# Lo parts of weights in a decoder layer: three FFN units by VectorE, two projection products by transfers within the chip

## The chip, the cores and the metric

The kernel runs on one core of a Trainium2 chip. A core has a matrix engine (TensorE, PE in the profile; its weight loads are PEld), a vector engine (VectorE, DVE), a scalar engine (ScalarE, ACT), GpSimd (POOL) and SyncE (SP), and 16 transfer engines shared by all queues. Here SP issues plain loads, and POOL issues the transfers that add to what lies at their destination. Each engine works through its own instructions in order, and so does each queue. The metric is the device time of one execution in microseconds; the median of the runs is quoted.

## The reference

One decoder layer on x of 512 tokens x 1024, in float32:

```
u = rms_norm(h, ln_mix_pre);  proj = u @ w_in
merged = g0*(y_swa @ w_swa) + g1*(y_sb @ w_sb) + g2*(y_mem @ w_mem)
mix = merged @ w_out
h = h + rms_norm(mix, ln_mix_post)
u = rms_norm(h, ln_ffn_pre)
a = silu(u @ w_gate) * (u @ w_up)            # 1024 -> 2816
h = h + rms_norm(a @ w_down, ln_ffn_post)
```

The change lies in `mix = merged @ w_out` (1024 x 1024), in the two norms behind it, and in the first weights of `u @ w_gate`, `u @ w_up`.

## The kernel before

**Precision.** TensorE multiplies in a shorter float format (fp32r). Each operand is split into hi, its value cast to that format by ScalarE, and lo, the rest; a product is three matmuls (`mm3`, lines 175, 177, 178): hi x hi, and the two of hi and lo. `split` (lines 135, 136) makes hi with a ScalarE cast and lo with a VectorE subtraction. `split_dma` (lines 147 to 149) makes lo without VectorE: ScalarE casts hi and writes -hi into lo, and a transfer issued by POOL adds the weight to it, here read again from the weights in main memory.

**Seven products.** The large products use a Winograd form of Strassen's scheme: a 2 x 2 block product with seven instead of eight half-size products, named p1, p2, p5, p6, p3, p7, p4, with sums of weights and of activations as operands. Weight sums are formed by accumulating transfers (`wo_plus`, `g_plus`). Products share PSUM banks: p1, p6, p7, p4 add up in bank x; p5 and p3 in y; p2 has w. Between two of a bank, ScalarE copies the intermediate state (p1, p5, p6), and VectorE joins it with a later one (`mkp` in the trace).

**The projection stage** (`mix_mm`, `wo_split`; about 410 to 452 us). Each product is done for token halves i = 0, 1 (256 tokens: two tiles of 128), with 4 k x 3 matmuls of 512 columns. The weights' parts are wop7h, wop7l and so on; those of p6 and p3 lie in tiles named hi and lo. p2 and p3 get lo by `split_dma`, the others by `split`. The activations' parts (mah/mal, mbd, mqh/mql, mrh/mrl) come from VectorE and ScalarE too; VectorE also joins the branches (g) just ahead.

**The norms** (`mix(t)`, lines 1132 to 1141, per token tile t of 128). Two ScalarE squares with accumulation, products with a gain (mt), statistics on 128 x 1 operands (b_m, t_m, v_m, r_m), the residual (xr), two more squares, statistics again (b_h to r_h), and the result mt. They are written under a priority that moves them forward in the engines' orders. `turn(t)` transposes mt by TensorE (ut) and splits it into FFN operands B11, B21 (tiles 0, 1) and, with tiles 2 and 3, T1, N2, N22, T3, T4.

**The FFN's gate and up products** work on units (p, n): p one of seven products, n a pair of 128-column blocks. A unit is one weight load of 512 KB (gw), one hi/lo split of 128 x 1024 and 24 matmuls of 256 columns. The order begins (p1,0), (p2,0), (p1,1), (p1,2), (p2,1), (p2,2), (p5,0), (p6,0), (p5,1), (p3,0). Unit (p1,0) is split by VectorE; the next three, (p2,0), (p1,1), (p1,2), by `split_dma` (`f_split_dma`, set as the unit's "way"). Their transfers share POOL's queue with the sums of weights of p5, p6 and p3 (`g_plus`, line 1246), which wait for their loads and for each other.

**What sets the order.** A scheduler orders each engine's instructions from the program's order, priorities and its own view of the dependences. `after(x, y)` pins x behind y on the same engine without a semaphore; `behind` pins later casts and subtractions to a given pair.

Of the kernel before, what the change touches and what calls it, by code (L numbers as in the profile page):

```python
# [17 lines left out]
P = 128  # L18
# [14 lines left out]
class Stream:  # L33
# [24 lines left out]
    def ahead(self, load_to, split_to):  # L58
        while self.loaded <= min(load_to, len(self.units) - 1):
            u = self.units[self.loaded]  # L60
            for fn in u["load"]:
                fn()
            u["raw"] = u["src"]() if callable(u["src"]) else self.load(u["src"], u["n"])
            self.loaded += 1
        while self.have <= min(split_to, len(self.units) - 1):
            u = self.units[self.have]
            for fn in u["split"]:
                fn()
            u["hl"] = u.get("way", self.split)(u["raw"], u["n"])
            self.have += 1  # L70

    def later(self, us, fn):
# [31 lines left out]
def tile_kernel(ctx, tc, a):  # L104
# [27 lines left out]
    def split(raw, hi, lo, sign=1.0):  # L132

        if sign == 1.0:
            ins = nc.scalar.copy(hi, raw)  # L135
            lows = nc.vector.tensor_tensor(lo, raw, hi.bitcast(F32), op=ALU.subtract)  # L136
        else:
            ins = nc.scalar.mul(hi, raw, sign)
            lows = nc.vector.scalar_tensor_tensor(lo, raw, sign, hi.bitcast(F32), op0=ALU.mult, op1=ALU.subtract)
        if "behind" in st:  # L140
            after(ins, st["behind"][0])
            after(lows, st["behind"][1])
        return ins

    def split_dma(raw, hi, lo, src):
# [114 lines left out]
    def parts(name, t):  # L260
        h, l = ck(f"{name}h", F32R), ck(f"{name}l", F32R)
        split(t[:, :], h[:, :], l[:, :])
        return h, l
# [325 lines left out]
    def branch(b, c2, order):  # L589
        def gen(hi, lo):  # L590
            for i in range(2):
                c = 2 * c2 + i
                g = st[(f"g{b}", c)] if (f"g{b}", c) in st else quart[(b, c)]
                ps = dps(f"br{b}{c}")
                for k in range(4):
                    mm3(ps[:, :], cols((hi, lo), (i * 4 + k) * P, P), y[(b, k)], k == 0, k == 3)
                    yield 0.65
                with tc.high_priority():
                    nc.vector.tensor_tensor(g[:, :], ps[:, :], g[:, :], op=ALU.mult)
                if order == 0:  # L600
                    st[("acc", c)] = g
                    continue
                acc = st[("acc", c)]
                if order == 1:
                    nc.vector.tensor_tensor(acc[:, :], acc[:, :], g[:, :], op=ALU.add)
                    continue
                nc.vector.tensor_tensor(acc[:, :], acc[:, :], g[:, :], op=ALU.add)
                merged[c] = acc
                if c < 4:
                    if c % 2 == 0:  # L610
                        ma.append((ck(f"mah{c}", F32R), ck(f"mal{c}", F32R)))
                    sl = slice((c % 2) * 256, (c % 2) * 256 + 256)
                    split(acc[:, :256], ma[-1][0][:, sl], ma[-1][1][:, sl])
                    continue
                mbd.append(parts(f"mbd{c}", acc))
                nc.vector.tensor_tensor(acc[:, 256:], merged[c - 4][:, 256:], acc[:, 256:], op=ALU.subtract)

        return gen
# [423 lines left out]
    def wo_split(p, key, k):  # L1042
        if p not in ("p6", "p3"):
            hl = tuple(ck(f"wo{p}{x}{k}", F32R)[:, :] for x in "hl")
        else:
# [1 line left out]
                uid[0] += 1  # L1047
                st["wo_two"] = [wp.tile([P, 1024], F32R, tag=x, name=f"{x}{uid[0]}", bufs=4) for x in ("hi", "lo")]
            hl = tuple(x[:, (k % 2) * 512 : (k % 2) * 512 + 512] for x in st["wo_two"])
        if p in ("p2", "p3"):  # L1050
            j, h = (1, 0) if p == "p2" else (1, 1)
            split_dma(wsum[key][k][:, :], *hl, a["w_out"][:, h, 4 * j + k])
        else:
            split(wsum[key][k][:, :], *hl)
        wt[(p, k)] = hl

    def rstd_small(name, ss):
# [456 lines left out]
    for k in range(4):  # L1514
        wo_split("p6", "r", k)
    wo_plus("r", 1, 0)
    for i in range(2):
        mix_mm("p2", i)
    for k in range(4):
# [2 lines left out]
    mix_mm("p5", 0)  # L1522
    mix_mm("p6", 0)
    for k in range(4):
        wo_split("p7", "b", k)
        turned_d(k)
    mix_mm("p5", 1)
    mix_mm("p3", 0)
    table("natural_log_exp_and_others")
    with tc.high_priority():  # L1530
        tmp[0] = mix(0)
    for k in range(4):
        wo_split("p4", "r", k)
    for p, i in (("p6", 1), ("p7", 0), ("p3", 1)):
        mix_mm(p, i)
    first.close()
# [2 lines left out]
    def f_split(raw, n):  # L1539
# [5 lines left out]
                split(x[:, :], hi[:, i * 512 : (i + 1) * 512], lo[:, i * 512 : (i + 1) * 512])  # L1545
        else:
            split(raw[:, :n], hi[:, :n], lo[:, :n])
        return hi, lo

    def f_split_dma(raw, src):  # L1550
        uid[0] += 1
        hi = fp.tile([P, 1024], F32R, tag="hi", name=f"hi{uid[0]}", bufs=4)
        lo = fp.tile([P, 1024], F32R, tag="lo", name=f"lo{uid[0]}", bufs=4)
        split_dma(raw[:, :], hi[:, :], lo[:, :], src)
        return hi, lo

    fs = Stream(None, f_split, LOAD_AHEAD + 1)
# [44 lines left out]
            tmp[t] = mix(t)  # L1602

    mixed(1)
    for i, (p, n) in enumerate(seq[:4]):
        if i > 0:
            fs.units[i]["way"] = lambda raw, w, n=n, j=(0 if p == "p1" else 1): f_split_dma(raw, g_src(n, 0, j))
    fs.ahead(3, 0)
    mix_mm("p4", 0)
    mixed(2)  # L1610
    mix_mm("p7", 1)
    turn(0, tmp[0])
    fs.ahead(4, 3)
    mix_mm("p4", 1)
    turn(1, tmp[1])
    mixed(3)
# [116 lines left out]
```

## Time and profile before

| what | us |
|---|---|
| runs shown | 813.27, 814.96, 815.26 (median 814.96) |
| the profiled execution | 813.38 |
| its span, first to last instruction | 811.6 |
| TensorE busy in the span | 784.5 |
| VectorE busy | 630.6 |
| ScalarE busy | 474.9 |
| POOL busy | 103.4 |
| mean granted TensorE clock | 0.984 of full |

Rows of the time line read: start, duration, engine, line of the kernel, operation, output <- inputs, shapes, count of merged instructions, and in brackets the idle time of the engine before and what ended it. Rows of waits read: engine, line and what waited <- what was waited for: total us, times, longest. Rows of stretches (a:b) give length, then busy us and count for PE, PEld, DVE, ACT, POOL, the granted clock, the busy share of the transfer engines (up to rounding errors above 1) and GB/s. Durations of pipelined matmuls overlap; the distance of their starts is what each takes. Rows of transfers end with the median us from issue to landing, or with minimum, median and maximum. The profiled time, 813.38, is 1.58 below the median of the runs; sums made on the trace are compared with it.

### The profile page before, as it was taken

The page shows a single profiled execution, that of the slowest core. Times are in us where ns is not written, and L with a number is a line of the kernel's source. Part 1 is how long each engine was busy: PE and PEld are TensorE (multiplying, and loading weights), DVE is VectorE, ACT ScalarE, POOL GpSimd, SP SyncE. Part 2 cuts the span into 40 slices and gives each one's busy share as a digit, 9 for nine tenths or more (in the row PEclk, how much of TensorE's full clock was granted, in tenths as well). Part 3 has the DMA queues.
Part 4 walks back from the last instruction along what each step waited for, and adds up shares of the span by engine and source line. Part 5 has one row for each costly group of instructions (what it writes and reads, how often), then busy time and mean ns, then how long its engine had stood idle before and what let it go on. Part 6 is the DMA issues. An engine that isn't in the chain of part 4 may idle for free.

```text
span 811.6 us, 12844 instructions
## 1 busy us (share of the span) xinstructions
PE 784.5 (97%) x4851; PEld 697.1 (86%) x4851; DVE 630.6 (78%) x999; ACT 474.9 (59%) x879; POOL 103.4 (13%) x130
## 2 busy tenths in 40 slices
PE   9999999999999999999999649999999999999996
PEld 6899887877888898899877549999999999988885
DVE  6898976844688796977688749977676767898797
ACT  7566755644655566656846837545555555666673
POOL 1102110000000001001560120110000000205200
PEclk9999999999999999999999769999999999999999
DMA  8343355222324027258993994987767762759902
GB/s 297 131 149 102 117 187 177 73 83 58 102 76 105 27 64 222 41 140 271 188 241 93 312 194 120 290 229 199 190 178 189 180 173 89 173 134 220 214 0 104
DMA packets 46334, 124.37 MB, mean 153 GB/s; under 512 B 5152, under 2 KB 7088, under 8 KB 46272
## 3 DMA queue, kind: packets, MB, share of 16 engines
q1 hardware_dynamic: 32448, 86.66, 33.0%
q0 software_dynamic: 13536, 36.69, 24.2%
q8 instruction: 38, 0.62, 0.3%
q10 hardware_dynamic: 288, 0.20, 0.1%
q14 instruction: 24, 0.20, 0.1%
HBM read 119.86 MB, written 3.67 MB: 152 GB/s over the span
## 4 chain that ended last, share of the span: by engine, by line
PE 90%; DVE 3%; issue 3%; DMA 2%; POOL 1%; ACT 0%; SPq 0%; DVEq 0%; POOLq 0%; ACTq 0%
PE gx L178 5%; PE gx L175 5%; PE gx L177 5%; PE g L175 3%; PE g L178 3%; PE br L177 3%; PE br L175 3%; PE g L177 3%; PE br L178 3%; PE gy L178 3%; PE gy L177 3%; PE gy L175 3%; PE x L175 2%; PE x L178 2%; PE x L177 2%
## 5 line engine op out<-in xcount | busy, mean ns | idle before, releaser
L135 ACT CAST hi<-gw 128x1024 fp32r<-128x1024 f32 x74 | 77.0, 1050 | 76.5 <-DVE gw L1264 36.0
L136 DVE TENSOR_TENSOR lo<-gw,hi 128x1024 fp32r<-128x1024 f32 x74 | 89.9, 1224 | 33.9 <-ACT hi L135 33.9
L135 ACT CAST hi<-raw 128x1024 fp32r<-128x1024 f32 (+2 forms) x52 | 53.9, 1042 | 51.9 <-PE g L177 13.7
L136 DVE TENSOR_TENSOR lo<-raw,hi 128x1024 fp32r<-128x1024 f32 (+2 forms) x52 | 62.9, 1215 | 19.0 <-ACT hi L135 18.8
L1246 POOL DMA_DIRECT2D gw<-in_w_gu x27 | 23.8, 906 | 201.8 <-DMA gw<-in_w_gu 75.8
L178 PE MATMUL gx<-B11h,lo 128*128 128x256 f32 x88 | 26.8, 304 | 10.7 <-DMA lo<-in_w_gu 10.7
L135 ACT CAST hi<-r 128x1024 fp32r<-128x1024 f32 (+1 forms) x24 | 23.6, 983 | 19.8 <-PE y L178 5.3
L177 PE MATMUL x<-lo,lh 128*128 128x512 f32 x88 | 34.2, 389 | 0.0
L175 PE MATMUL x<-hi,lh 128*128 128x512 f32 x88 | 34.2, 389 | 0.0
L178 PE MATMUL x<-hi,ll 128*128 128x512 f32 x88 | 34.1, 389 | 0.0
L838 DVE TENSOR_TENSOR_SCAN p<-r,anew 128x512 f32<-128x512 f32 (+1 forms) x24 | 24.7, 1041 | 8.1 <-ACT r L195 7.6
L175 PE MATMUL gx<-B11h,hi 128*128 128x256 f32 x88 | 26.9, 306 | 3.9 <-ACT B11h L1175 3.9
L136 DVE TENSOR_TENSOR lo<-r,hi 128x1024 fp32r<-128x1024 f32 (+1 forms) x24 | 27.2, 1133 | 3.9 <-ACT hi L135 3.7
L135 ACT CAST hi<-qw 128x1024 fp32r<-128x1024 f32 x18 | 18.9, 1052 | 16.1 <-PE g L177 3.7
L136 DVE TENSOR_TENSOR lo<-qw,hi 128x1024 fp32r<-128x1024 f32 x18 | 22.0, 1222 | 8.2 <-ACT hi L135 8.2
L178 PEld LDWEIGHTS gx<-B11h,lo 128*128 128x128 f32 x88 | 18.6, 212 | 10.9 <-DMA lo<-in_w_gu 10.9
L135 ACT CAST hi<-bp 128x512 fp32r<-128x512 f32 x33 | 19.2, 621 | 13.5 <-PE y L178 4.8
L177 PE MATMUL gx<-B11l,hi 128*128 128x256 f32 x88 | 26.6, 303 | 0.0
L136 DVE TENSOR_TENSOR lo<-bp,hi 128x512 fp32r<-128x512 f32 x33 | 22.4, 714 | 4.6 <-ACT hi L135 4.4
L175 PE MATMUL gw<-B21h,hi 128*128 128x256 f32 x88 | 25.1, 285 | 0.0
L178 PE MATMUL gy<-N22h,lo 128*128 128x256 f32 x88 | 25.0, 284 | 0.0
L175 PE MATMUL gx<-T4h,hi 128*128 128x256 f32 x88 | 25.0, 284 | 0.0
(1024 smaller groups left out, 2979.5 us busy)
## 6 DMA issues: line engine op xcount, KB each, us to landing
gw<-in_w_gu SPq DMA_DIRECT2D x57, 512.0 KB, 5.4
gw<-in_w_gu POOLq DMA_DIRECT2D x27, 512.0 KB, 7.3
raw<-in_w_p SPq DMA_DIRECT2D x26, 512.0 KB, 4.0
qw<-in_w_p SPq DMA_DIRECT2D x15, 512.0 KB, 3.9
raw<-in_w_br SPq DMA_DIRECT2D x12, 512.0 KB, 3.8
bp<-in_w_dn SPq DMA_DIRECT2D x22, 256.0 KB, 8.5
r<-in_w_dn POOLq DMA_DIRECT2D x10, 512.0 KB, 8.4
qw<-in_w_p POOLq DMA_DIRECT2D x6, 512.0 KB, 7.5
```

Source lines behind the costliest of these rows:

```text
L135: ins = nc.scalar.copy(hi, raw)
L136: lows = nc.vector.tensor_tensor(lo, raw, hi.bitcast(F32), op=ALU.subtract)
L175: one = nc.tensor.matmul(out, lh, rh, start=start, stop=False, skip_group_check=True)
L177: nc.tensor.matmul(out, *two, start=False, stop=False, skip_group_check=True)
L178: st["product"] = nc.tensor.matmul(out, *three, start=False, stop=stop, skip_group_check=True)
L838: ins = nc.vector.tensor_tensor_scan(p[:, :w], left1[i][:, :w], anew[:, o : o + w], 0.0, op0=ALU.mult, op1=ALU.max)
L1246: nc.gpsimd.dma_start(gw[(n, key)][:, :], g_src(n, i, j), accum_op=ALU.add)
```

## The change

- The three FFN units (p2,0), (p1,1), (p1,2) are split by `split`: ScalarE casts hi, VectorE subtracts. While they are written, `st["late"]` holds the last instruction of the second token tile's norm, and the three subtractions are pinned behind it. `f_split_dma` and the units' own "way" are gone.
- Projection products p7 and p4: lo by `split_dma`, but the transfer reads the weight sum that already lies on the chip (SBUF to SBUF). p7's split is written ahead of p2's products and p4's ahead of tile 0's norm; before, both came behind.
- p2's lo goes from a transfer to VectorE. p3 keeps its transfer from main memory.
- p6's four splits are pinned behind the last split of the merged branches (`st["seam"]`, the pair for mbd7).

```diff
@@ class Stream, ahead
-            u["hl"] = u.get("way", self.split)(u["raw"], u["n"])
+            u["hl"] = self.split(u["raw"], u["n"])
@@ split
             after(lows, st["behind"][1])
+        if "late" in st:
+            after(lows, st["late"])
+        st["both"] = (ins, lows)
         return ins
@@ branch
                 mbd.append(parts(f"mbd{c}", acc))
+                st["seam"] = st["both"]
@@ wo_split
-        if p in ("p2", "p3"):
-            j, h = (1, 0) if p == "p2" else (1, 1)
-            split_dma(wsum[key][k][:, :], *hl, a["w_out"][:, h, 4 * j + k])
+        if p in ("p7", "p4"):
+            split_dma(wsum[key][k][:, :], *hl, wsum[key][k][:, :])
+        elif p == "p3":
+            split_dma(wsum[key][k][:, :], *hl, a["w_out"][:, 1, 4 + k])
         else:
             split(wsum[key][k][:, :], *hl)
+            if p == "p6":
+                for x, y in zip(st["both"], st["seam"]):
+                    after(x, y)
@@ the projection stage
     wo_plus("r", 1, 0)
+    for k in range(4):
+        wo_split("p7", "b", k)
     for i in range(2):
         mix_mm("p2", i)
...
     for k in range(4):
-        wo_split("p7", "b", k)
         turned_d(k)
     mix_mm("p5", 1)
     mix_mm("p3", 0)
     table("natural_log_exp_and_others")
+    for k in range(4):
+        wo_split("p4", "r", k)
     with tc.high_priority():
         tmp[0] = mix(0)
-    for k in range(4):
-        wo_split("p4", "r", k)
@@ the FFN's first units
     mixed(1)
-    for i, (p, n) in enumerate(seq[:4]):
-        if i > 0:
-            fs.units[i]["way"] = lambda raw, w, n=n, j=(0 if p == "p1" else 1): f_split_dma(raw, g_src(n, 0, j))
+    late = st["mixed"]
     fs.ahead(3, 0)
     mix_mm("p4", 0)
     mixed(2)
     mix_mm("p7", 1)
     turn(0, tmp[0])
+    st["late"] = late
     fs.ahead(4, 3)
+    st.pop("late")
```

The engines' orders move at three places. First POOL's queue between the projection and the FFN; wor and wob are the projection's weight sums, gw the FFN's weights, lo its lo parts. Before:

```order
L1040 DMA wor3_3924<-in_w_out 128x512
L1246 DMA gw147_4783<-in_w_gu 128x1024
L149 DMA lo156_4892<-in_w_gu 128x1024
L1246 DMA gw148_4785<-in_w_gu 128x1024
L1246 DMA gw149_4787<-in_w_gu 128x1024
L1246 DMA gw148_4785<-in_w_gu 128x1024
L1246 DMA gw153_4884<-in_w_gu 128x1024
L1246 DMA gw149_4787<-in_w_gu 128x1024
L149 DMA lo157_4897<-in_w_gu 128x1024
L149 DMA lo158_4902<-in_w_gu 128x1024
```

Now:

```order
L1044 DMA wor3_3924<-in_w_out 128x512
L152 DMA wop7l0_4525<-wob0_4190 128x512
L152 DMA wop7l1_4530<-wob1_4191 128x512
L152 DMA wop7l2_4535<-wob2_4192 128x512
L152 DMA wop7l3_4540<-wob3_4193 128x512
L152 DMA wop4l0_4651<-wor0_3921 128x512
L152 DMA wop4l1_4656<-wor1_3922 128x512
L152 DMA wop4l2_4661<-wor2_3923 128x512
L152 DMA wop4l3_4666<-wor3_3924 128x512
L1254 DMA gw147_4787<-in_w_gu 128x1024
L1254 DMA gw148_4789<-in_w_gu 128x1024
```

The three transfers of FFN lo parts are gone, and eight transfers of the projection stand ahead of all the FFN's sums.

Second VectorE's order around tile 0's norm. mkp60 and mkp61 are the joins of p3 for token halves 0 and 1, mkp50 that of p7 for half 0; mt, b_m, v_m, t_m, r_m, xr are the norm. Before:

```order
L136 TENSOR_TENSOR wop7l3_4616<-wob3_4193,wop7h3_4615 128x512
L1120 TENSOR_TENSOR mkp60_4595<-my0_4568,mkp60_4595 128x512
L1134 TENSOR_TENSOR mt01_4653<-mkp60_4595,bc_g_post1_4311 128x512
L1134 TENSOR_TENSOR mt00_4652<-mkp10_4439,bc_g_post0_4310 128x512
L1061 TENSOR_SCALAR b_m0_4658<-ssm0_4650 128x1
L136 TENSOR_TENSOR wop4l0_4685<-wor0_3921,wop4h0_4684 128x512
L1063 SCALAR_TENSOR_TENSOR v_m0_4659<-ssm0_4650,b_m0_4658 128x1
L136 TENSOR_TENSOR wop4l1_4689<-wor1_3922,wop4h1_4688 128x512
L136 TENSOR_TENSOR wop4l2_4693<-wor2_3923,wop4h2_4692 128x512
L1065 SCALAR_TENSOR_TENSOR t_m0_4660<-r_m0_4661,v_m0_4659 128x1
L136 TENSOR_TENSOR wop4l3_4697<-wor3_3924,wop4h3_4696 128x512
L1123 TENSOR_TENSOR mkp50_4581<-mkp50_4581,mx0_4426 128x512
```

Now:

```order
L136 TENSOR_TENSOR mrl3_4487<-g13_1866,mrh3_4486 128x256
L1128 TENSOR_TENSOR mkp60_4611<-my0_4584,mkp60_4611 128x512
L1131 TENSOR_TENSOR mkp50_4597<-mkp50_4597,mx0_4422 128x512
L1142 TENSOR_TENSOR mt01_4673<-mkp60_4611,bc_g_post1_4307 128x512
L1142 TENSOR_TENSOR mt00_4672<-mkp10_4435,bc_g_post0_4306 128x512
L1069 TENSOR_SCALAR b_m0_4678<-ssm0_4670 128x1
L1071 SCALAR_TENSOR_TENSOR v_m0_4679<-ssm0_4670,b_m0_4678 128x1
L1073 SCALAR_TENSOR_TENSOR t_m0_4680<-r_m0_4681,v_m0_4679 128x1
L1128 TENSOR_TENSOR mkp61_4716<-my1_4621,mkp61_4716 128x512
L1074 SCALAR_TENSOR_TENSOR r_m0_4681<-t_m0_4680,r_m0_4681 128x1
L1145 SCALAR_TENSOR_TENSOR xr00_4492<-mt00_4672,r_m0_4681,xr00_4492 128x512
```

The eight subtractions of wop7l and wop4l are gone; the join of p7 stands ahead of both mt products, and the join of p3's second half within the statistics. On TensorE p3 and p6 have changed places: p6's second half now comes ahead of p3's first. On ScalarE the eight casts and negations of p7 stand ahead of the copies of p5 and p6, and those of p4 ahead of tile 0's squares.

Third VectorE's order behind tile 1's norm, in tile 2's norm; B11l and B21l are FFN operands, lo156 to lo158 the lo parts of the three FFN units. Before:

```order
L1141 SCALAR_TENSOR_TENSOR mt11_4748<-xr11_4501,r_h1_4770,bc_g_fpre1_4317 128x512
L1176 TENSOR_TENSOR B11l0_3614<-ut00_4862,B11h0_3613 128x2x128
L1063 SCALAR_TENSOR_TENSOR v_m2_4824<-ssm2_4815,b_m2_4823 128x1
L1176 TENSOR_TENSOR B11l0_3614<-ut10_4918,B11h0_3613 128x2x128
L1065 SCALAR_TENSOR_TENSOR t_m2_4825<-r_m2_4826,v_m2_4824 128x1
L1066 SCALAR_TENSOR_TENSOR r_m2_4826<-t_m2_4825,r_m2_4826 128x1
L1176 TENSOR_TENSOR B11l1_3616<-ut00_4862,B11h1_3615 128x2x128
L1137 SCALAR_TENSOR_TENSOR xr20_4504<-mt20_4817,r_m2_4826,xr20_4504 128x512
```

Now:

```order
L1184 TENSOR_TENSOR B11l0_3614<-ut00_4866,B11h0_3613 128x2x128
L1071 SCALAR_TENSOR_TENSOR v_m2_4828<-ssm2_4819,b_m2_4827 128x1
L136 TENSOR_TENSOR lo156_4896<-gw146_4785,hi156_4895 128x1024
L1073 SCALAR_TENSOR_TENSOR t_m2_4829<-r_m2_4830,v_m2_4828 128x1
L1184 TENSOR_TENSOR B11l1_3616<-ut00_4866,B11h1_3615 128x2x128
L1074 SCALAR_TENSOR_TENSOR r_m2_4830<-t_m2_4829,r_m2_4830 128x1
L136 TENSOR_TENSOR lo157_4900<-gw150_4793,hi157_4899 128x1024
L1145 SCALAR_TENSOR_TENSOR xr20_4500<-mt20_4821,r_m2_4830,xr20_4500 128x512
L1145 SCALAR_TENSOR_TENSOR xr21_4501<-mt21_4822,r_m2_4830,xr21_4501 128x512
L1184 TENSOR_TENSOR B21l0_3618<-ut01_4867,B21h0_3617 128x2x128
L1069 TENSOR_SCALAR b_h2_4841<-ssh2_4820 128x1
L136 TENSOR_TENSOR lo158_4904<-gw151_4801,hi158_4903 128x1024
```

Two of the three new subtractions stand ahead of tile 2's residual (xr) and one within its second statistics; the part of B11 for the second token tile (B11l0 from ut10) has moved behind all three.

More of the change, by code (lines that the diff above doesn't have):

```diff
@@ L1547, in f_split @@
             split(raw[:, :n], hi[:, :n], lo[:, :n])
[L1548 to L1554, printed above, removed]
         return hi, lo
```

## The prediction

> **What bounds the kernel now.** I read the page first, then the waits of TensorE over the whole span, then the stretch with the largest wait in order of time.
>
> ```profile
> span 811.6 us, 12844 instructions
> PE 784.5 (97%) x4851; PEld 697.1 (86%) x4851; DVE 630.6 (78%) x999; ACT 474.9 (59%) x879; POOL 103.4 (13%) x130
> ...
> PE gx L178 <- DMA lo<-in_w_gu: 10.7, 1, 10.7
> PE gx L175 <- ACT B11h L1175: 3.9, 1, 3.9
> PE ut L1187 <- DVE mt L1141: 2.6, 2, 1.3
> ```
>
> TensorE is busy for 784.5 of 811.6 us, so only its waits and its slow stretches can be won. One wait of 10.7 us is larger than all others together: the third matmul of the FFN's unit (p1,1) waits for a lo part that comes by an accumulating transfer. In order of time, TensorE and then POOL's queue:
>
> ```profile
> 469.67 0.28 PE L177 MATMUL gx<-B11l,hi 128*128 128x256 f32 x1
> 480.62 0.58 PE L178 MATMUL gx<-B11h,lo 128*128 128x256 f32 x1 [10.67 <-DMA lo<-in_w_gu]
> 481.00 0.42 PE L175 MATMUL gx<-B11h,hi 128*128 128x256 f32 x1
> 486.48 0.36 PE L175 MATMUL gx<-B11h,hi 128*128 128x256 f32 x1
> 486.80 0.28 PE L178 MATMUL gx<-B11h,lo 128*128 128x256 f32 x1
> ...
> 466.37 1.75 POOL L1246 DMA_DIRECT2D gw<-in_w_gu  x2 [14.34 <-DMA gw<-in_w_gu]
> 470.21 2.09 POOL L149 DMA_DIRECT2D lo<-in_w_gu  x2
> ```
>
> The two late lo transfers stand in POOL's queue behind a weight sum that waits 14.34 us, are issued at 470.21, and the first lands when the matmul starts, at 480.62. After the wait the matmuls start 0.21 us apart until 486.48 (0.42 us each) and 0.12 us apart afterwards (0.28 us each). So the wait also costs about 23 matmuls x 0.09 = 2.1 us of slow clock.
>
> The Trainium skill (TensorE: Matmul & The Clock Gate, Part 1: The HAM clock gate) puts the fall to half clock after some 3.4 us without work and the return after as much work; the trace agrees in direction, with 5.9 us from 480.62 to 486.48. By that rule alone every new wait of several us ahead of the FFN would bring such a stretch again.
>
> **The change, part by part.** *FFN lo parts.* Three transfers of 512 KB and three ScalarE negations go; VectorE gets three subtractions instead.
>
> ```profile
> 447.89 1.06 ACT L148 ACTIVATE lo<-hi 128x1024 fp32r<-128x1024 f32 x1
> L136 DVE TENSOR_TENSOR lo<-gw,hi 128x1024 fp32r<-128x1024 f32 x74 | 89.9, 1224 | 33.9 <-ACT hi L135 33.9
> lo<-in_w_gu POOLq DMA_DIRECT2D x3, 512.0 KB, 12.4
> ```
>
> ScalarE loses 3 x 1.06, VectorE gains 3 x 1.22 (1.13 from start to start where instructions follow each other), and all three stand, by the order, inside token tile 2's norm. That takes the 10.7 us wait away, but what comes next is VectorE's chain of norms, to which the other edits add too.
>
> *Lo parts of p7 and p4 by transfers inside the chip.* VectorE loses 8 subtractions of 128x512, 0.69 us each by the row of that shape at 466.03 below. ScalarE gains 8 negations, and each product waits for four transfers of 256 KB. TensorE's dates for p7 and p4, and ScalarE's and the transfers' rows:
>
> ```profile
> 429.27 0.41 ACT L135 CAST mqh<-g 128x256 fp32r<-128x256 f32 x1 [1.26 <-DVE g L1092]
> 430.54 2.20 ACT L135 CAST wop7h<-wob 128x512 fp32r<-128x512 f32 x4
> 437.14 0.39 PE L175 MATMUL mx<-wop7h,mrh 128*128 128x512 f32 x1
> 442.58 0.39 PE L175 MATMUL mx<-wop4h,mbd4h 128*128 128x512 f32 x1
> DMA to landing us min/median/max: 4.3/6.4/6.6
> DMA to landing us min/median/max: 5.4/7.5/10.7
> 428.00:436.00 8.00, 8.00 (x35) 6.57 (x36) 6.10 (x14) 4.55 (x11) 0.00 (x0) 1.00 0.30 59
> 436.00:444.00 8.00, 8.00 (x37) 6.63 (x36) 7.25 (x18) 5.84 (x18) 0.00 (x0) 1.00 0.06 7
> ```
>
> The two landing rows are those of wop2l and of wob, 256 KB each. No transfer from SBUF to SBUF is in the trace. The nearest rows bound its landing by 4.3 and 10.7 us, and the long ones were taken where the transfer engines were full; here they stand at 0.30 and 0.06 of their time. I take 5.4. Then: ScalarE's last mqh, now near 429.9, ends at 430.2; four pairs of a cast (2.20 / 4) and a negation (half of 1.06, at half the width), together about 1.05 us, end at 431.3 to 434.4; the last lo lands at 439.8. TensorE, 0.9 us later than before (next edit), needs it for its fourth k, at 437.14 + 0.9 + 3 x 0.68 + 0.23 = 440.3 (12 matmuls are 2.72 us: p7,0 begins at 437.14, and p4 two products later at 442.58). p4's pairs follow three copies of about 0.5 us and end at 440.2; landing 445.6, needed at 442.58 + 0.9 + 2.27 = 445.75. Both are in time by tenths only: at the low bound (4.3) nothing changes, at 10.7 p7's k = 3 is 4.8 us late. The negations also hold back the copy of p5's bank, which p3 overwrites; the new order runs p6,1 ahead of p3,0, and the copy ends at 435.0 for a start of p3,0 at 435.3.
>
> The Trainium skill (DMA: Bandwidth & Descriptors, Anatomy of one DMA) gives about 2.0 us plus bytes at 436 GB/s, an estimate of 2.6 us for 256 KB. No row here is as short, and by that figure p7 and p4 would have 3 us to spare.
>
> *p6 behind the seam, p2 by VectorE.* p2's four subtractions (2.4 us in all) fall between 390 and 400, and cost nothing as long as VectorE is idle there; without that cover they would cost 2.4. p6's pin moves two of its four subtractions into a full stretch:
>
> ```profile
> 395.00:400.00 5.00, 5.00 (x24) 4.14 (x23) 3.78 (x8) 5.00 (x11) 4.39 (x6) 1.00 1.07 194
> 427.94 0.50 PE L178 MATMUL mx<-hi,mrl 128*128 128x512 f32 x1 [0.25 <-DVE mrl L136]
> ```
>
> VectorE already sets the pace there (TensorE waits 0.25 us for its mrl). Two subtractions of 0.60 from start to start more, and one of them offset by mbd5l having run earlier, makes TensorE 0.6 to 1.2 us late; I take 0.9, on every date up to 448.
>
> *The chain of norms.* These rows give its dates before; the sum is the walk of the new order with their durations.
>
> ```profile
> 436.23 1.29 DVE L1134 TENSOR_TENSOR mt<-mkp,bc_g_post 128x512 f32<-128x512 f32 x2 [0.92 <-ACT mt L1132]
> 440.90 1.41 DVE L1137 SCALAR_TENSOR_TENSOR xr<-mt,r_m,xr 128x512 f32<-128x512 f32 x2
> 448.03 1.03 PE L1187 MATMUL ut<-c_ident,mt 128*128 128x128 f32 x8
> 449.27 1.42 DVE L1137 SCALAR_TENSOR_TENSOR xr<-mt,r_m,xr 128x512 f32<-128x512 f32 x2
> 461.55 0.58 PE L175 MATMUL gx<-B11h,hi 128*128 128x256 f32 x1 [3.93 <-ACT B11h L1175]
> 461.67 1.40 DVE L1141 SCALAR_TENSOR_TENSOR mt<-xr,r_h,bc_g_fpre 128x512 f32<-128x512 f32 x2
> 466.03 0.69 DVE L1134 TENSOR_TENSOR mt<-mkp,bc_g_post 128x512 f32<-128x512 f32 x1 [1.27 <-ACT mt L1132]
> 471.71 1.42 DVE L1141 SCALAR_TENSOR_TENSOR mt<-xr,r_h,bc_g_fpre 128x512 f32<-128x512 f32 x2
> 476.04 0.42 DVE L1274 TENSOR_TENSOR aq<-gp,sg 128x256 f32<-128x256 f32 x1
> 486.32 0.69 DVE L1196 TENSOR_TENSOR t<-ut,ur 128x512 f32<-128x512 f32 x1 [9.86 <-PE ut L1187]
> 503.24 2.36 DVE L136 TENSOR_TENSOR lo<-gw,hi 128x1024 fp32r<-128x1024 f32 x2
> 504.51 0.39 PE L178 MATMUL gy<-N22h,lo 128*128 128x256 f32 x1
> ```
>
> Tile 0: VectorE now has p7's join ahead of the two mt products, so these wait for p7,0's end, 437.14 + 12 matmuls x 0.227 (439.86) + 0.9 and a handover: join 441.0, mt 441.6 instead of 436.23; the join of p3,1 falls in between too, and xr starts at 444.6 instead of 440.9. Though eight subtractions left this stretch, tile 0 is 3.7 us later. Tile 1: the join of p7,1 (TensorE done near 448.9) stands ahead of its statistics; xr at 452.8 instead of 449.27, 3.5 later. Tile 2: two new lo parts stand ahead of its xr and one behind, 3 x 1.13 = 3.4, of which about 1.7 is new waiting; its mt ends near 468.3 instead of 463.07, 5.2 later. Tile 3: before, it began at 466.03, 3.0 us behind tile 2's mt, since it waited for ScalarE; that slack takes up 2.4 of the 5.2, and mt ends at 475.9 instead of 473.13, 2.8 later.
>
> TensorE's first FFN unit goes on at about 466.3 instead of 461.55, 4.8 later, and, without the 10.7 us wait, its last transposes (ut of tile 3) done near 478.5 instead of 486.48: 8.0 us earlier. VectorE has, between mt of tile 3 and the first step behind those transposes, 3.3 us of work (473.13 to 476.46 before, inside the wait of 9.86), so it starts that step at 475.9 + 3.3 = 479.2 instead of 486.32: 7.1 us earlier. From there VectorE was full up to the lo part that ends at 504.4, for which TensorE's matmul at 504.51 waited a tenth. So VectorE binds, and the gain is its 7.1 us and not TensorE's 8.0. Behind 504 nobody in TensorE's row waits and all moves along.
>
> Sum against the profiled execution's own 813.38 us (span 811.6): 10.7 + 2.1 won, 4.8 given back because the FFN's first units start later, 0.9 more because VectorE and not TensorE sets the pace behind them (rounding 0.1): 7.1, so 806.3. The median of the three runs shown is 814.96, 1.6 above the profiled one; on it 807.9, and I predict **808**.
>
> **The rivals.** *The on-chip lo parts land late* (as wob's did: median 7.5, longest 10.7 us, in the row above). p7's margin of 0.5 us makes 5.9 the landing from which it decides; each us more is a us for TensorE, then for tile 0's norm and all behind it. At 7.5 it costs 1.6, at 10.7 4.8, and the result is 809.5 to 812.7. For it: the margins of tenths; four transfers in flight at once. Against it: transfer engines nearly idle.
>
> *VectorE does not bind.* If mt of tile 3 ends as early as before, 473.1, VectorE starts at 476.4 and 9.9 us are won: 805; if TensorE also keeps its clock, all of 12.8: 802. Against it is the order, which puts lo parts and joins ahead of the norms.
>
> *Slower.* One mechanism: the transfers inside the chip take as long as the FFN's did (12.4, the row above, though for 512 KB). p7's last k is then 12.4 - 5.9 = 6.5 us late. p4's lands at 440.2 + 12.4 = 452.6, needed, with p7's delay, at 445.75 + 6.5 = 452.25: 0.4 more. If the wait also lets the clock fall as before (2.1), that is 9.0 against the 7.1 won: 817. It decides from a landing of about 12.6 us without, or 10.5 with, the slow clock. Queueing on POOL, one after the other, would have to do this.
>
> *The wait only changes its name.* If a later FFN unit then waits for its weight sums, the dates stay: 815.
>
> ```profile
> 478.37 1.75 POOL L1246 DMA_DIRECT2D gw<-in_w_gu  x2 [6.06 <-DMA gw<-in_w_gu]
> gw<-in_w_gu POOLq DMA_DIRECT2D x8, 512.0 KB, 8.8
> 501.51 1.05 ACT L135 CAST hi<-gw 128x1024 fp32r<-128x1024 f32 x1
> ```
>
> Against it: even unmoved the last two sums of the first seven products land near 479.2 + 8.8 = 488, and ScalarE takes unit (p3,0)'s weights at 501.51, so 7.1 earlier at 494.4.
>
> **How the numbers follow.** 0.3%, 2.4 us, is about what a measurement here can tell from no change. Forecast 0.57 (own range 805 to 811: 0.9 and 5.4 at their bounds and 1.5 us of error in each norm); late transfers 0.18; VectorE free 0.12; slower 0.06; renamed 0.07. Faster than 812.5: 0.55 + 0.14 + 0.12 = 0.81; slower than 817.4: 0.04 of the slower case and 0.03 of the renamed one, which would add this change's lost tenths; within: the other 0.12. The range that leaves out 2 in 10 reaches from 803.5, inside the free case, to 813, past the late transfers.
>
> **What would show it.** Right: no wait on DMA lo in TensorE's waits; ut of tile 3 near 478; mt of tile 0 at about 441.6 behind the join of p7; waits of TensorE of some us on mt and B11 between 453 and 468; VectorE full from 479. Wrong: a wait of TensorE on the transfers wop7l or wop4l (the late rival); mt of tile 3 ending before 474 (VectorE free); a wait on weight sums before 500 (renamed); waits behind 504, which my walk assumes away.

## The result, and the profile after

The changed kernel takes 804.03 us (median of 4 runs, 803.20 to 804.67), the kernel before 814.12 us in its 4 runs (812.46 to 815.26). The ratio is 0.9877, with a 95% interval from 0.9855 to 0.9899. The forecast was 808, with a range from 803.5 to 813: the sign and the range hold, and the gain of some 10 us is larger than the 7.1 of the sum. The time lies only 0.5 us above the lower end of the range, which was there for a rival (VectorE does not bind), and below the 805 to 811 that the forecast gave for its own mechanism.

The profiled execution is the one of 804.03 us. From its page, the span, the busy times and the chain that ended last:

```profile
span 802.2 us, 12855 instructions
PE 782.9 (98%) x4851; PEld 695.0 (87%) x4851; DVE 631.1 (79%) x998; ACT 474.7 (59%) x880; POOL 103.4 (13%) x131
PE 89%; DVE 7%; ACT 2%; issue 2%; DVEq 0%; ACTq 0%
```

What TensorE waited for over the whole span (engine, line, what waited <- what for: total us, times, longest):

```profile
PE ut L1195 <- DVE mt L1149: 4.0, 2, 2.8
PE gx L180 <- DVE B11l L1184: 3.2, 1, 3.2
PE gw L178 <- ACT B21h L1183: 1.9, 1, 1.9
```

The wait of 10.7 us on a transfer is gone. No transfer stands in TensorE's list; what is left between 452 and 464 are waits for the norms: for mt, which is to be transposed, and for the FFN operands made from it. The chain that ended last runs, outside TensorE, through VectorE (7%) and ScalarE (2%), and no transfer stands in it.

TensorE in order of time: p7's first matmul, the FFN's first steps, and tile 3's transposes.

```profile
436.07 0.39 PE L178 MATMUL mx<-wop7h,mrh 128*128 128x512 f32 x1
463.51 0.58 PE L180 MATMUL gx<-B11l,hi 128*128 128x256 f32 x1 [3.17 <-DVE B11l L1184]
467.01 0.28 PE L180 MATMUL gx<-B11l,hi 128*128 128x256 f32 x1
474.49 1.04 PE L1195 MATMUL ut<-c_ident,mt 128*128 128x128 f32 x8
```

p7,0 starts 1.07 us earlier than before (437.14), where the prediction had it 0.9 later. The first FFN units go on at 463.51, 2.0 later than before (461.55), not 4.8. From there to 467.01 the matmuls start 0.21 us apart, afterwards 0.12. Tile 3's transposes begin at 474.49; in the kernel before they began at 485.48, 11.0 us later, and the prediction had them near 478.

VectorE's dates for the norms (tile 0's mt products, xr of tiles 0 and 1, the results mt of tiles 2 and 3, and the first step t behind tile 3's transposes):

```profile
439.59 1.29 DVE L1142 TENSOR_TENSOR mt<-mkp,bc_g_post 128x512 f32<-128x512 f32 x2
442.52 1.41 DVE L1145 SCALAR_TENSOR_TENSOR xr<-mt,r_m,xr 128x512 f32<-128x512 f32 x2
450.65 1.41 DVE L1145 SCALAR_TENSOR_TENSOR xr<-mt,r_m,xr 128x512 f32<-128x512 f32 x2
463.78 1.41 DVE L1149 SCALAR_TENSOR_TENSOR mt<-xr,r_h,bc_g_fpre 128x512 f32<-128x512 f32 x2
472.96 1.42 DVE L1149 SCALAR_TENSOR_TENSOR mt<-xr,r_h,bc_g_fpre 128x512 f32<-128x512 f32 x2
477.63 0.68 DVE L1204 TENSOR_TENSOR t<-ut,ur 128x512 f32<-128x512 f32 x1
493.86 2.36 DVE L136 TENSOR_TENSOR lo<-gw,hi 128x1024 fp32r<-128x1024 f32 x2
```

| date on VectorE, us | before | predicted | measured |
|---|---|---|---|
| mt products of tile 0 | 436.23 | 441.6 | 439.59 |
| xr of tile 0 | 440.90 | 444.6 | 442.52 |
| xr of tile 1 | 449.27 | 452.8 | 450.65 |
| mt of tile 2, end | 463.07 | 468.3 | 465.2 |
| mt of tile 3, end | 473.13 | 475.9 | 474.4 |
| first step t behind tile 3's transposes | 486.32 | 479.2 | 477.63 |

Every norm came later than before, as forecast, and every one 1.5 to 3.1 us earlier than forecast. The step t starts without any wait, 3.1 us after TensorE began the transposes for it. VectorE is late there, not TensorE. The step is 8.7 us earlier than before; the lo parts that ended before's chain at 503.24 start at 493.86, 9.4 us earlier, and 9.4 is what the span lost (811.6 to 802.2).

### The profile page after: what moved, and what is told of

It reads as the page before. It is cut to its first block, busy times and chain, and to the rows that moved or that the text cites. A ratio compares the mean times of both kernels' runs of the same rounds, so it can differ in the third digit from the quotient of the medians.

```text
span 802.2 us, 12855 instructions
## 1 busy us (share of the span) xinstructions
PE 782.9 (98%) x4851; PEld 695.0 (87%) x4851; DVE 631.1 (79%) x998; ACT 474.7 (59%) x880; POOL 103.4 (13%) x131
## 4 chain that ended last, share of the span: by engine, by line
PE 89%; DVE 7%; ACT 2%; issue 2%; DVEq 0%; ACTq 0%
PE gx L178 5%; PE gx L181 5%; PE gx L180 5%; PE g L178 3%; PE g L181 3%; PE g L180 3%; PE gy L178 3%; PE gy L181 3%; PE gy L180 3%; PE br L178 3%; PE br L180 2%; PE br L181 2%; PE x L178 2%; PE x L181 2%; PE x L180 2%
## 5 line engine op out<-in xcount | busy, mean ns | idle before, releaser
L135 ACT CAST hi<-gw 128x1024 fp32r<-128x1024 f32 x77 | 79.8, 1047 | 77.0 <-DVE gw L1272 36.5
L136 DVE TENSOR_TENSOR lo<-gw,hi 128x1024 fp32r<-128x1024 f32 x77 | 93.5, 1223 | 34.0 <-ACT hi L135 34.0
L135 ACT CAST hi<-bp 128x512 fp32r<-128x512 f32 x33 | 19.3, 620 | 13.4 <-PE y L181 4.8
L181 PE MATMUL gy<-T1h,lo 128*128 128x256 f32 x88 | 25.0, 284 | 0.8 <-DVE lo L136 0.8
L387 POOL DMA_DIRECT2D qw<-in_w_p x6 | 7.3, 1211 | 140.0 <-DMA qw<-in_w_p 46.6
L178 PE MATMUL gy<-T1h,hi 128*128 128x256 f32 x88 | 25.0, 284 | 0.2 <-ACT hi L135 0.2
```

The lines of the kernel that those rows point to most:

```text
L178: one = nc.tensor.matmul(out, lh, rh, start=start, stop=False, skip_group_check=True)
L181: st["product"] = nc.tensor.matmul(out, *three, start=False, stop=stop, skip_group_check=True)
L387: nc.gpsimd.dma_start(raw[:, :].rearrange("p (g m) -> p g m", g=2), q_src(b, n, f, j), accum_op=ALU.add)
```

## The experiments

Eleven more kernels ran. One number orders them: the date of VectorE's step t, 477.63 in the rows above. The table gives the median, the ratio to the kernel before measured beside it (its medians were 814.12, 813.13, 813.93 and 813.34), the span of the profiled run and that date. The ratios of the change, e1, e4, e5 and e7 lie within each other's intervals: what sets these five apart is read from their traces, one for each kernel, and not from their times.

| kernel | median us | ratio, 95% interval | span | step t | span - t |
|---|---|---|---|---|---|
| before | 814.12 | 1 | 811.6 | 486.32 | 325.3 |
| the change | 804.03 | 0.9877 [0.9855, 0.9899] | 802.2 | 477.63 | 324.6 |
| e1: FFN part alone | 803.61 | 0.9884 [0.9867, 0.9901] | 801.9 | 477.27 | 324.6 |
| e2: projection part alone | 810.73 | 0.9977 [0.9963, 0.9990] | 809.7 | 484.38 | 325.3 |
| e3: change without the seam pin | 806.30 | 0.9916 [0.9899, 0.9933] | 804.7 | 480.07 | 324.6 |
| e4: change, p7 and p4 by VectorE | 802.53 | 0.9873 [0.9854, 0.9892] | 800.4 | 475.79 | 324.6 |
| e5: change without the late pin | 804.83 | 0.9891 [0.9869, 0.9913] | 803.8 | 479.18 | 324.6 |
| e6: change, three lo parts twice | 807.82 | 0.9925 [0.9906, 0.9944] | 805.6 | 480.96 | 324.6 |
| e7: before, sums behind lo | 803.45 | 0.9884 [0.9859, 0.9908] | 801.7 | 477.08 | 324.6 |
| e9: e4's projection with e7's queue | 801.34 | 0.9849 [0.9827, 0.9871] | 799.5 | 474.88 | 324.6 |
| e10: e9, first unit by transfer too | 805.25 | 0.9898 [0.9879, 0.9917] | 804.2 | 478.93 | 325.3 |
| e11: e9, lo read on the chip | 801.50 | 0.9854 [0.9839, 0.9870] | 799.8 | 475.21 | 324.6 |
| e12: e10 and e11 | 803.66 | 0.9883 [0.9862, 0.9904] | 800.7 | 475.01 | 325.7 |

In nine kernels, spread over 6 us, the span is the date of t plus 324.6 us to a few hundredths. In the four others TensorE is the late one: in before, e2 and e10 VectorE's step waits for the transposes, and in e12, although the step does not wait, TensorE waits for nothing behind 475.

### Which part of the change brings the gain (e1, e2)

e1 makes only the FFN edit: the three units go back to `split`, pinned behind `late`; p2, p6, p7 and p4 stay as in the kernel before.

```diff
+        if "late" in st:
+            after(lows, st["late"])
...
-    for i, (p, n) in enumerate(seq[:4]):
-        if i > 0:
-            fs.units[i]["way"] = lambda raw, w, n=n, j=(0 if p == "p1" else 1): f_split_dma(raw, g_src(n, 0, j))
+    late = st["mixed"]
...
+    st["late"] = late
     fs.ahead(4, 3)
+    st.pop("late")
```

> The kernel before with the FFN part of the change alone: lo parts of (p2,0), (p1,1), (p1,2) by VectorE behind the second norm; the projection stays as it was. Theory: the wait of 10.7 us on lo goes, and VectorE's norms set what follows; in the changed kernel tile 1's residual starts at 450.65 against 449.27 before, so without the projection edits the norms are some 1.4 us earlier and the time is about 802.6. Rival (the projection edits carry part of the gain by freeing VectorE and by the earlier TensorE): 805 to 807.

e2 is the opposite: the changed kernel, with the three FFN lo parts by transfers as before.

> The changed kernel with the FFN's three lo parts given back to transfers: only the projection edits are left. Theory: TensorE waits about 10 us for the FFN's lo as before, whatever the projection does ahead of it, so 812.5 to 815, like the kernel before. Rival (the projection edits are worth something by themselves, by an earlier TensorE or fewer VectorE steps): 811 or less.

Waits of TensorE in e1, and its step t on VectorE in order of time:

```profile
PE gx L180 <- DVE B11l L1179: 3.2, 1, 3.2
PE mw L178 <- ACT mbd7h L135: 0.7, 1, 0.7
PE mw L181 <- DVE mbd6l L136: 0.5, 1, 0.5
```

```profile
477.27 0.68 DVE L1199 TENSOR_TENSOR t<-ut,ur 128x512 f32<-128x512 f32 x1
```

TensorE's wait in e2 and POOL's issue of the two lo transfers, in order of time on each engine:

```profile
478.87 0.58 PE L181 MATMUL gx<-B11h,lo 128*128 128x256 f32 x1 [7.63 <-DMA lo<-in_w_gu]
469.95 2.09 POOL L152 DMA_DIRECT2D lo<-in_w_gu  x2
```

The FFN edit alone gives the whole gain: ratios of 0.9884 and 0.9877, spans of 801.9 and 802.2. The projection edits then add nothing. It is a little slower than the 802.6 expected: the waits at the seam are there (0.7 and 0.5 us, rows two and three), and p7,0 starts at 438.17, 2.1 us later than in the changed kernel. That is also 1.0 later than in the trace of the kernel before, from which the 802.6 was worked out, though the projection stage is the same in both.

Alone, the projection edits are worth 0.23% (0.9963 to 0.9990), some 2 us, which is the rival's result (811 or less) and not the theory's. The wait on lo is 7.6 instead of 10.7 us. Of these 3.0 us, 1.3 are no gain: TensorE only comes to the wait later (471.24 against 469.95). The other 1.75 are the landing, at 478.87 instead of 480.62. The lo transfers are issued at the same time as before (469.95 against 470.21) and land earlier. The sums ahead of them in the queue were issued some 4 us earlier (462.10 against 466.37), which leaves less in flight beside them; that this is the reason is argued, not shown.

### The seam pin (e3)

```diff
             split(wsum[key][k][:, :], *hl)
-            if p == "p6":
-                for x, y in zip(st["both"], st["seam"]):
-                    after(x, y)
```

> The changed kernel without the pin of p6's splits behind the seam. Theory after the result: the pin took away TensorE's waits of 0.65, 0.22 and 0.25 us between 418 and 428, because the splits no longer stand ahead of mbd4 to mbd7; without it they come back, p7,0 starts about 1.1 us later, and so does all behind it: 805.1. The prediction on record had the pin cost 0.9: then 803.1.

Rows of TensorE in e3, in order of time:

```profile
419.60 0.50 PE L178 MATMUL mw<-wop2h,mbd7h 128*128 128x512 f32 x1 [0.69 <-ACT mbd7h L135]
420.56 0.50 PE L181 MATMUL mw<-wop2h,mbd7l 128*128 128x512 f32 x1 [0.22 <-DVE mbd7l L136]
428.67 0.50 PE L181 MATMUL mx<-hi,mrl 128*128 128x512 f32 x1 [0.26 <-DVE mrl L136]
435.62 0.50 PE L178 MATMUL my<-hi,mqh 128*128 128x512 f32 x1 [0.28 <-ACT mkp L1119]
438.52 0.39 PE L178 MATMUL mx<-wop7h,mrh 128*128 128x512 f32 x1
```

Without the pin p7,0 starts at 438.52 instead of 436.07, 2.45 us later, and the span is 2.5 us longer. The sign is that of the theory and against the prediction; the size is twice the 1.1 expected. The first three waits are those of the kernel before, whose first two rows are these (the third, at 427.94, stands in the prediction):

```profile
418.89 0.50 PE L175 MATMUL mw<-wop2h,mbd7h 128*128 128x512 f32 x1 [0.65 <-ACT mbd7h L135]
419.84 0.50 PE L178 MATMUL mw<-wop2h,mbd7l 128*128 128x512 f32 x1 [0.22 <-DVE mbd7l L136]
```

The last two of e3 are in the changed kernel too, as matmuls of 0.5 us at 425.90 and 433.20, with less idle time. Each wait also costs a few tenths beside the idle time shown: by the distances of starts the four cost 2.6 us in e3, and the two that are left cost 0.6 in the changed kernel. That is 1.9 of the 2.45 us; the rest was not followed.

What the pin moves out of the way is seen on ScalarE, first two rows of the kernel before, then one of the changed kernel:

```profile
407.90 0.62 ACT L135 CAST hi<-wor 128x512 fp32r<-128x512 f32 x1 [3.70 <-DMA wor<-in_w_out]
411.63 0.61 ACT L135 CAST mbd4h<-g 128x512 fp32r<-128x512 f32 x1
```

```profile
405.53 0.62 ACT L135 CAST mbd4h<-g 128x512 fp32r<-128x512 f32 x1 [1.70 <-DVE g L610]
```

In the kernel before p6's first cast waits 3.70 us for its weight sum to land, its second (411.10) another 2.58, and mbd4's cast stands behind both: it starts at 411.63 instead of 405.53, though its input was there at 404.88. VectorE, whose subtractions stand in the same order, idles 2.51 us for p6's hi (to 408.55) and 1.33 for mbd4h (to 412.28). In e3 the two casts wait 2.74 and 3.17 us, and mbd4's starts at 411.24. So the pin wins because ready work no longer stands behind work that waits for a transfer.

The stage varies from trace to trace, but by less than the pin wins. With the projection of the kernel before, p7,0 starts at 437.14 (before), 438.17 (e1) and 437.87 (e7); with that of the changed kernel at 436.07, 436.26 (e2), 435.77 (e5) and 435.80 (e6). So the pin wins some 2.5 us in this kernel, and it pays for the rest of the projection edits: with them but without the pin, p7,0 is 0.4 to 1.4 us later than in the first three.

### Transfers inside the chip (e4)

```diff
-        if p in ("p7", "p4"):
-            split_dma(wsum[key][k][:, :], *hl, wsum[key][k][:, :])
-        elif p == "p3":
+        if p == "p3":
             split_dma(wsum[key][k][:, :], *hl, a["w_out"][:, 1, 4 + k])
```

> The changed kernel with p7's and p4's lo by VectorE at the same place in the program, no transfers inside the chip. Theory: VectorE was idle for 7.13 us ahead of 436.34 and the four subtractions of p7 fit in there, p4's into the gap behind; ScalarE loses eight negations (5.0 us), so tile 0's squares start earlier and its products are done about 1.7 us earlier; 802.3 to 803. Rival (what the change is for: VectorE is the bound, eight subtractions more delay the norms): 805 to 807.

VectorE ahead of tile 0's norm, first in the changed kernel, then in e4:

```profile
436.34 0.69 DVE L1128 TENSOR_TENSOR mkp<-my,mkp 128x512 f32<-128x512 f32 x1 [7.13 <-PE my L181]
```

```profile
435.33 0.69 DVE L1126 TENSOR_TENSOR mkp<-my,mkp 128x512 f32<-128x512 f32 x1 [2.41 <-PE my L181]
436.88 1.30 DVE L1140 TENSOR_TENSOR mt<-mkp,bc_g_post 128x512 f32<-128x512 f32 x2 [0.26 <-ACT mt L1138]
438.09 0.68 DVE L1129 TENSOR_TENSOR mkp<-mkp,mx 128x512 f32<-128x512 f32 x1
475.79 0.69 DVE L1202 TENSOR_TENSOR t<-ut,ur 128x512 f32<-128x512 f32 x1
```

The transfers took eight subtractions away from a VectorE that stood idle for 7.13 us there. Back on VectorE they use up that idle time, ScalarE does no negations, the mt products stand at 436.88 instead of 439.59 and ahead of p7's join again, and step t is 1.8 us earlier. Half of this is there before tile 0's norm: p7,0 starts at 435.13, 0.9 us earlier. The rest goes with ScalarE's negations and the place of the join, which were not taken apart. The time is 802.5, within the theory's 802.3 to 803, but the ratio, 0.9873 against 0.9877, does not tell the two kernels apart. The transfers were nearly in time, and nothing shows that they were worth having.

### Who binds behind the norms (e5, e6)

e5 leaves out the pin of the three subtractions behind `late`. e6 does each of them twice:

```diff
         if "late" in st:
             after(lows, st["late"])
+            again = nc.vector.tensor_tensor(lo, raw, hi.bitcast(F32), op=ALU.subtract)
+            after(again, lows)
+            lows = again
```

> The changed kernel without the pin behind the second norm: by the order the three new subtractions then stand inside tile 1's norm. Theory (VectorE's chain from tile 0 to the step behind tile 3's transposes sets the end, so it matters little in which norm the 3.4 us stand, but tile 1's result and with it TensorE's first FFN matmuls come 2 to 3 us later): 804 to 806.5. Rival (the pin does nothing, or the place of the subtractions decides): 802 or less, or above 807.

> The changed kernel with each of the three new subtractions done twice into the same place (3 x 1.13 us more on VectorE, nothing more for anyone else). Theory (VectorE sets the pace from the norms to 504): tile 3's norm waits 1.43 us for ScalarE, which takes up part, so 2.0 to 3.4 us more than the changed kernel: 806 to 807.4. Rival (TensorE, which waits little behind 477, sets the end): 804 to 804.6.

The first row of TensorE's waits in e5, e5's step t, and e6's step t:

```profile
PE ut L1195 <- DVE mt L1149: 9.4, 2, 8.1
```

```profile
479.18 0.68 DVE L1204 TENSOR_TENSOR t<-ut,ur 128x512 f32<-128x512 f32 x1
```

```profile
480.96 0.68 DVE L1207 TENSOR_TENSOR t<-ut,ur 128x512 f32<-128x512 f32 x1
```

In e6, 3.4 us more on VectorE make the step 3.3 us later and the span 3.4 us longer; the median of 807.8 is 0.4 above the theory's upper end. So more work on VectorE here moves the end, and nothing in tile 3's slack takes this up: the wait of 1.43 us for ScalarE there is as long as in the changed kernel. In e5 tile 1's results come 4 to 5 us later (last mt at 459.92 against 455.80), more than the 2 to 3 expected; TensorE waits 8.1 us at once for them, and yet the step is only 1.6 us later (804.8, as the theory had it). TensorE's own waits there cost little; the date of VectorE's step counts.

### Was it the transfer or its place in the queue (e7)

e7 is the kernel before with its three lo transfers. The second round of weight sums, which add to tiles whose first sum must have landed, is written after them and pinned behind them.

```diff
-        nc.gpsimd.dma_start(lo, src, accum_op=ALU.add)
+        st["lo_dma"] = nc.gpsimd.dma_start(lo, src, accum_op=ALU.add)
...
-        nc.gpsimd.dma_start(gw[(n, key)][:, :], g_src(n, i, j), accum_op=ALU.add)
+        ins = nc.gpsimd.dma_start(gw[(n, key)][:, :], g_src(n, i, j), accum_op=ALU.add)
+        if "lo_dma" in st and n < 2:
+            after(ins, st["lo_dma"])
...
-        ("p5", 1, 1), ("p6", 1, 1), ("p3", 1, 1), ("p6", 0, 0), ("p3", 0, 0), ("p3", 0, 1)
+        (3, "p5", 1, 1), (3, "p6", 1, 1), (3, "p3", 1, 1), (5, "p6", 0, 0), (5, "p3", 0, 0), (5, "p3", 0, 1)
```

The new first number is the unit at whose load the sum is written; the sum for "t" is moved from 4 to 5 as well.

> The kernel before, with its three lo transfers kept, but the second round of weight sums pinned behind them in POOL's queue. Theory: the lo transfers were late only because they stood behind a sum that waited 14.34 us; issued at about 461 they land by 469 to 473, the wait of 10.7 us goes, VectorE keeps the dates it had before (tile 3's mt at 473.1, 3.3 us of work behind it), so 9.9 us are won against the kernel before: 803 to 804, as good as the changed kernel. Rival (transfers of 512 KB land 10 to 12 us after issue however they are queued): a wait of 2 to 4 us and the slow clock are left, 806 to 809.

POOL's queue and TensorE in e7, in order of time; then the landing of lo, from its tile's view:

```profile
457.48 0.86 POOL L149 DMA_DIRECT2D lo<-in_w_gu  x1 [4.90 <-ACT r_m L195]
461.88 0.86 POOL L149 DMA_DIRECT2D lo<-in_w_gu  x1 [3.55 <-ACT r_h L195]
466.78 0.86 POOL L1246 DMA_DIRECT2D gw<-in_w_gu  x1 [4.04 <-DMA gw<-in_w_gu]
472.34 0.39 PE L178 MATMUL gx<-B11h,lo 128*128 128x256 f32 x1 [0.56 <-DMA lo<-in_w_gu]
```

```profile
DMA to landing us min/median/max: 12.9/13.0/14.8
```

The landing is as long as before (13.0, before 12.4 us). Issued at 457.48 and 461.88 instead of 470.21, the transfers are in time all but 0.56 us, and the kernel takes 803.5 us. A matter of order in one queue was worth the whole change (ratios of 0.9884 and 0.9877), with no work moved to VectorE. The rival was right that the landing stays long, longer even than its 10 to 12 us, but its wait of 2 to 4 us did not come.

### The two put together, and further (e9 to e12)

e9 has the projection of e4 (seam pin, p7 and p4 by VectorE) and the queue of e7. e10 also gives the first unit, (p1,0), to `f_split_dma` (`if i >= 0`); e11 is e9 with `raw[:, :]` on the chip as the source of the lo transfers; e12 is both.

> Parts combined: projection with p6 behind the seam and p7, p4 by VectorE (the 802.5 us version), but the FFN's three lo parts by transfers that stand ahead of the second round of weight sums. Theory (VectorE's norms set the end): 3.4 us fewer on VectorE in tile 2's norm, of which the 1.43 us slack of tile 3 hides a part; 799.5 to 801. Rival (lo lands late, or TensorE's own work sets the end now): 802 to 804.

> The 801.3 us version, with the lo part of the first FFN unit (p1,0) by a transfer too, so that its subtraction leaves tile 1's norm. Theory: the time follows VectorE's date for the first step behind tile 3's transposes plus 324.6 us; 1.1 us fewer ahead of it: 800 to 800.6. Rival (this lo, needed first, lands 13 us after its issue near 447, behind TensorE's first FFN matmuls): 801.5 or more, with a wait on lo ahead of 465.

> The 801.3 us version, with the FFN's lo transfers reading the weights from the chip instead of main memory. If it is the source that makes them slow (the on-chip transfers of the projection, half the size, landed in 4.0 us), they land in 6 to 9 us and the wait of 0.85 us on lo goes; if it is the company of the other loads (transfer engines full at 452 to 470), they land in 11 to 13 us as before. The time stays at 801 to 801.6 in both cases, since VectorE sets the end.

> Both at once: first unit's lo by a transfer too, and all four read from the chip. By the theory 800 to 800.6 as for the first unit alone; less than that only if a faster landing also lets TensorE's first FFN unit start earlier; 801.5 or more if lo is late all the same.

Step t of e9; then e10's largest waits of TensorE and its step t; then the landing of lo in e11:

```profile
474.88 0.68 DVE L1202 TENSOR_TENSOR t<-ut,ur 128x512 f32<-128x512 f32 x1
```

```profile
PE gx L181 <- DMA lo<-in_w_gu: 4.4, 1, 4.4
PE gw L181 <- DMA lo<-in_w_gu: 3.4, 1, 3.4
```

```profile
478.93 0.69 DVE L1202 TENSOR_TENSOR t<-ut,ur 128x512 f32<-128x512 f32 x1 [0.74 <-PE ut L1193]
```

```profile
DMA to landing us min/median/max: 11.6/13.4/14.6
```

e9 has the lowest time, 801.34 us, just above its theory's 799.5 to 801 (its interval, 0.9827 to 0.9871, and the changed kernel's overlap a little; the spans differ by 2.7 us). Against e4 it took 3.4 us of work from VectorE in tile 2's norm and won only 0.9 at step t. VectorE now waits there for ScalarE:

```profile
456.20 0.22 DVE L1071 SCALAR_TENSOR_TENSOR t_m<-r_m,v_m 128x1 f32<-128x1 f32 x1 [1.04 <-ACT r_m L198]
```

So the chain of norms runs through VectorE and ScalarE in turn. Work added to VectorE lengthens it (e6), but work taken away shortens it only until VectorE waits for ScalarE.

e10 met its rival: with a fourth transfer TensorE waits 4.4 and 3.4 us on lo again, TensorE is the late one, and 3.9 us are lost. e11 shows that it is not the source: read on the chip, lo lands in 13.4 us, as from main memory (13.0 in e9). e12 has e10's waits (3.8 and 2.8 us), and its runs spread from 802.5 to 805.4, none as low as the 800 to 800.6 of the theory.

## Why the prediction was right, and where it was off

**What bounds the kernel** was read rightly: the wait on lo was the matter, and it went. The new bound is the one forecast, VectorE's chain of norms; e6 and the constant 324.6 us show it. (e9 adds that ScalarE has its part in that chain.) The 3.3 us of work between tile 3's mt and step t were 3.25 (474.38 to 477.63).

**The step that failed** is "p6 behind the seam": forecast as 0.6 to 1.2 us later on every date up to 448, taken as 0.9. Against the same kernel without the pin it is 2.45 earlier (e3). The prediction counted the two subtractions that come into a full stretch and did not follow what comes out ahead of them: in the kernel before, two of p6's casts, which waited 3.70 and 2.58 us for their weight sums, stood in front of mbd4's, and TensorE later waited for mbd7's hi and lo (0.65 and 0.22 us; nearly the same rows stand in e3). p7,0 started at 436.07 instead of the 438.0 forecast. From there the dates stay ahead of the forecast: tile 0 by 2.0, tile 1 by 2.1, tile 2 by 3.1, tile 3 by 1.5 and step t by 1.6, which is most of the 2.3 us by which the sum of 7.1 fell short of 9.4. In the terms of that sum, TensorE's later start gave back 2.0 us instead of 4.8, and VectorE behind it 2.3 (11.0 less 8.7) instead of 0.9: two errors that offset each other in part.

**The rest of that gap** is "behind 504 all moves along". All does, but from a base that differs: where VectorE comes last, the end is 324.6 us after step t; where it waits for TensorE, as before the change, 325.3. That is 0.7 us more. Between 808 and 804.03 there are 1.6 us besides: the prediction added them because the median of the runs lay that far above the profiled execution. In the changed kernel the profiled execution is the median.

**Transfers inside the chip** were in time, as forecast, but for 0.28 us that the weight load of p4's last lo waited, at 443.79. They landed in 4.0 us for p7 and 4.1 for p4 (medians) where 5.4 was taken; the estimate of 2.6 us beside it was too short. That no row is as short holds for the transfers that add: plain stores of 256 KB (out) landed in 2.0 us. That the edit costs tile 0 more than the eight subtractions save was forecast too (join of p7 first, ScalarE busy with negations), and e4 puts a number on it: 1.8 us at step t. The cost of p2's subtractions, put at nothing while VectorE is idle there, was not measured apart: the projection edits without the pin make p7,0 0.4 to 1.4 us late, and p2's four subtractions may be part of it.

**The clock.** The Trainium skill (TensorE: Matmul & The Clock Gate, Part 1: The HAM clock gate) has the clock come back after some 3.4 us of work. Behind the waits that end with the one of 3.17 us the slow stretch lasted from 463.51 to 467.01, 3.5 us, which agrees; so does the 3.8 us of the kernel before behind its wait of 3.93 us (461.55 to 465.36). Its 5.9 us behind the wait of 10.67 are longer. The wait of 0.56 us in e7 brought none: from the second matmul behind it on they start 0.12 us apart. The stretch of 5.9 us is gone in the changed kernel, as the pace after 467 shows, and with it the 2.1 us of slow clock that the prediction counted.

**The rivals.** "VectorE does not bind" gave 805, and the time came out closer to it than to the forecast, but not by its mechanism: tile 3's mt ended at 474.4, not 473.1, and doing VectorE's new work twice moved the end by its full 3.4 us (e6). That the time came out at the lower edge of the range is due to the pin, about which no rival spoke: without it (e3) it is 806.3. Late on-chip transfers (but for the 0.28 us) and a renamed wait did not occur.

## What to carry to other kernels

Before an expensive transfer is replaced by engine work, look at what stands in front of it in its queue: here an accumulating transfer that waited for another's landing held two others, whose operands were ready, for 9 to 14 us (ready at 460.87 and 456.45, issued at 470.21), and changing their order gave as much as moving the work. The same holds for an engine's own order: two casts that waited for weight sums held mbd4's cast until 411.63. An engine is relieved only where it is busy: eight subtractions taken from a VectorE that was idle for 7 us, at the price of eight negations on ScalarE, made step t 1.8 us later. When a pin moves work, cost both ends: what it joins, and what it no longer stands in front of.

## What the hardware showed that was not expected

**Small on-chip transfers fill the transfer engines.** The same 10 us in the changed kernel and in e4, which differ for the transfer engines by eight transfers of 256 KB (columns: length; busy us and count of PE, PEld, DVE, ACT, POOL; clock; share of the transfer engines; GB/s):

```profile
430.00:440.00 10.00, 10.00 (x45) 7.99 (x44) 1.71 (x3) 9.81 (x21) 6.28 (x8) 1.00 0.99 168
```

```profile
430.00:440.00 10.00, 10.00 (x46) 8.29 (x45) 5.74 (x13) 4.86 (x12) 0.00 (x0) 1.00 0.03 12
```

They take the share from 0.03 to 0.99 at 168 GB/s, and each lands in about 4 us (3.6 to 4.5 for p7). Nothing else wanted the engines there.

**A subtraction on VectorE can take 2.6 times as long beside POOL's arithmetic.** In the changed kernel, two subtractions of one shape and form, the first under POOL's scaling of the gains, the second without:

```profile
406.99 1.75 DVE L136 TENSOR_TENSOR mbd4l<-g,mbd4h 128x512 fp32r<-128x512 f32 x1
407.23 3.32 POOL L1032 TENSOR_SCALAR bc_g_post<-bc_g_post 128x512 f32<-128x512 f32 x2
416.86 0.68 DVE L136 TENSOR_TENSOR mbd7l<-g,mbd7h 128x512 fp32r<-128x512 f32 x1
```

It takes 1.75 us instead of 0.68. The Trainium skill (SBUF — State Buffer, Who interferes with whom) names the shared port pair of VectorE and GpSimd as the only one that causes contention, and the row agrees. Not every subtraction is slowed: in e4 one of the same shape keeps its 0.68 us, and POOL's two scalings take 4.58 us instead of 3.32:

```profile
408.09 0.68 DVE L136 TENSOR_TENSOR mbd5l<-g,mbd5h 128x512 fp32r<-128x512 f32 x1
405.52 4.58 POOL L1032 TENSOR_SCALAR bc_g_post<-bc_g_post 128x512 f32<-128x512 f32 x2
```

The pin won although it brought mbd4's and mbd5's subtractions into this stretch.
